# Mixer A's left and right key blocks folded by a minimum ahead of exp and transposes, and put apart again by GpSimd

## The chip, the cores and the metric

The kernel runs on one core of a Trainium2 chip. The metric is device time in microseconds (us) of one execution, the median of several runs. Engines are named as in the profile: PE (TensorE, with its weight loads as PEld), DVE (VectorE), ACT (ScalarE), POOL (GpSimd) and SP (SyncE, which issues most DMAs).

## What is computed

Two layers on 1024 tokens of 1024 channels, all in float32. Layer 0 uses mixer A, 2-D neighbourhood attention; layer 1 uses mixer B, grouped-query attention. Each is followed by a gated output projection and a gated embedding. The change concerns mixer A:

```python
rs = np.clip(r - win_r // 2, 0, rows - win_r)        # 16 rows, window of 8
cs = np.clip(c - win_c // 2, 0, GRID_W - win_c)      # 64 columns, window of 16
...
sc = jnp.einsum('bhqd,bhqnd->bhqn', qb, kg) * scale
sc = sc + bb                                         # learned bias by 2-D offset
pr = jax.nn.softmax(sc, axis=-1)
return jnp.einsum('bhqn,bhqnd->bhqd', pr, vg)
```

Each query sees 8 rows x 16 columns of keys; there are 16 heads of width 64.

## The kernel before

The host lays the tokens out in 8 tiles of 128: a tile holds all 16 rows of 8 neighbouring columns. So a query tile j sees keys of the tiles j − 1, j and j + 1 (at the two edges, j = 0 and 7, of two tiles). Of the middle tile all 8 columns lie in the window; of the left tile those with c(key) >= c(query), of the right tile those with c(key) < c(query), where c is the column within the tile. For one query and one place within a tile, thus, either the left key or the right key counts, never both.

Products of weights and activations are split into a high and a low part (three matmuls each, the helper `split3`, recorded at L315 as are all matmuls of the helper `mm`).

Mixer A walks over 16 heads x 8 query tiles, 128 steps. A step's parts, by function:

- `f_S` (scores): two matmuls into PSUM (`s`), then one DVE instruction (L674) that adds the table `tb` (bias and mask, 1e30 where a key is out) and writes `sp`, with the row's minimum `mn`. Scores are negated, so a minimum is the largest score.
- `f_E` (exp, ACT, L683): `sp` becomes exp(mn − sp) in place, with the row sums.
- `f_T` (transposes): PE transposes each 128 x 128 block of `sp` (L691) into PSUM (`t`); ACT copies it to `PTh` (L694), DVE writes the remainder to `PTl` (L695). `PTh` and `PTl` have three slots for each key tile k, for the queries of tiles k − 1, k and k + 1: slots 3k, 3k + 1, 3k + 2.
- `f_AV` (product with v, by key tile kb): two matmuls, with PTh and with PTl, over the slots of kb, into `o`. It needs the transposes of query tile kb + 1.

In step n the order is: `f_T` of n, `f_E` of n + 1, `f_S` of n + 2, and `f_AV` of n − 2. When half of a head's products are done, `head_end` brings out `Y`, and four steps later POOL multiplies it with the gate `G` (L529) and with the reciprocal row sums `rb` (L530), which come through a DMA. POOL also makes each head's table `tb` from the mask `MK` and the bias rows `u` (L649, five products). In heads 3, 7 and 11 the projection of v for the next four heads goes beside the attention (`v_items`).

All engines run their queues in order. The order is written out in the program: `mix` deals the parts of attention (`att`, with the costs CA) and of dense projections (`dense`, the next head's q and k, the gates) onto PE's queue in proportion to given costs; `pulse` after each part lets weights be staged, split into high and low (`wh` by ACT at L225, `wl` by DVE at L230) and delayed small work be issued. `QS`, `KA`, `KB` (L618 to L627) are the next head's q and k, split by ACT and DVE.

Of the kernel before, what the change touches and what calls it, by code (L numbers as in the profile page):

```python
# [21 lines left out]
NT = 8  # L22
# [3 lines left out]
NH = 16  # L26
# [4 lines left out]
CA = (1.0, 0.5, 1.25, 1.0, 0.75)  # L31
# [56 lines left out]
def lay_out(inp):  # L88
    g = {k: np.asarray(v) for k, v in inp.items()}
    W = np.empty((len(UNIT), 128, 1024), np.float32)  # L90

    def put(keys, cols, per):
        blk = cols.reshape(cols.shape[0] // 128, 128, -1).transpose(1, 0, 2)
        for u, key in enumerate(keys):
            W[UNIT[key]] = blk[:, u * per:(u + 1) * per].reshape(128, -1)

    aq, ak, av, ag = np.split(g["a_w_in"][0], 4, axis=1)
    for h in range(16):
        s = slice(h * HD, (h + 1) * HD)
        put([("aqk", h)], np.concatenate([aq[:, s], ak[:, s]], axis=1), 8)  # L100
    for q in range(4):
        put([("av", q, 0), ("av", q, 1)], av[:, q * 256:(q + 1) * 256], 4)
    bw = g["b_w_in"][0]
    bq, bk, bv, bg = bw[:, :1024], bw[:, 1024:1280], bw[:, 1280:1536], bw[:, 1536:]
    for p in range(8):
        s = slice(p * 128, (p + 1) * 128)
        put([("ag", p)], ag[:, s], 8)
        put([("bg", p)], bg[:, s], 8)
    for i in range(4):
        put([("bq", i, 0), ("bq", i, 1)], bq[:, i * 256:(i + 1) * 256], 4)  # L110
    for i in range(2):
# [24 lines left out]
    mask = np.where(ok, 0.0, BIG).astype(np.float32)  # L136

    inv = np.power(np.float32(10000.0), -np.arange(16, dtype=np.float32) * np.float32(2.0) / np.float32(32.0)).astype(np.float32)
# [12 lines left out]
    return {  # L151
        "x": tokens(g["x"][0]), "wts": W, "rpb": rpb, "gains": gains, "hgains": hg,
        "mask": mask, "rope": np.stack([cosT, sinT], axis=1),
        "gain0": gains[0].reshape(8, 128).T,
    }


@with_exitstack
def trunk(ctx, tc, x, wts, rpb, gains, hgains, mask, rope, gain0, out):
    nc = tc.nc  # L160
    sync, act, dve, pool, pe = nc.sync, nc.scalar, nc.vector, nc.gpsimd, nc.tensor

# [6 lines left out]
    ident = glob.tile([128, 128], F32, name="ident")  # L169
# [406 lines left out]
    def mixer_a():  # L576
        with ExitStack() as es:
# [4 lines left out]
            sb = es.enter_context(tc.tile_pool(name="asb", bufs=2))  # L582
            V = one.tile([128, NT, 4, 128], F32R, name="V")
            MK = one.tile([128, 5, 128], F32, name="MK")

            def dalloc():
                return pd.tile([128, 512], F32, name="d")
# [66 lines left out]
            def near(j):  # L654
                return max(j - 1, 0), min(j + 1, NT - 1)

            def f_S(h, j):
# [12 lines left out]
                else:  # L670
# [4 lines left out]
                                         in0=ps[:, :n].rearrange("p (k c) -> p k c", c=128), in1=tb,  # L675
                                         scale=1.0, scalar=1e38, op0=ALU.add, op1=ALU.min, accum_out=mn)
                SP[h, j] = (sp, mn)

            def f_E(h, j):
                k0, k1 = near(j)  # L680
                n = (k1 - k0 + 1) * 128
                sp, mn = SP[h, j]
                act.activation(sp[:, :n], sp[:, :n], AF.Exp, bias=mn, scale=-1.0, accum_out=RS[h][:, j:j + 1])  # L683

            def f_T(h, j):
                k0, k1 = near(j)
                m = k1 - k0 + 1
                sp, _ = SP.pop((h, j))
                ps = psT.tile([128, 4, 128], F32, name="t")
                for i in range(m):  # L690
                    pe.transpose(ps[:, i], sp[:, i * 128:(i + 1) * 128], ident)  # L691
                f0 = k0 * 3 + (j - k0 + 1)
                sl = slice(f0, f0 + 2 * m - 1, 2)
                act.activation(PTh[:, sl], ps[:, :m], AF.Copy)  # L694
                dve.tensor_tensor(PTl[:, sl], ps[:, :m], PTh[:, sl], ALU.subtract)  # L695

            def talloc():
                return psT.tile([128, 4, 128], F32, name="t")
# [122 lines left out]
            vs[1][1]()  # L821
            newton(4)
            sync.dma_start(MK, mask)
            for c in range(8):
                sync.dma_start(U[:, c], rpb[:, :, 7 - c:31 - c])
            for t in range(2, NT):
# [27 lines left out]
            PTh = ptp.tile([128, NT * 3, 128], F32R, name="PTh")  # L854
            PTl = ptp.tile([128, NT * 3, 128], F32R, name="PTl")
            for d in qk_items(0):
                d[0]()
                WQ.pump()
# [18 lines left out]
            for h in range(NH):  # L877
                att = []
                for j in range(NT):
# [22 lines left out]
                dense = []  # L902
                if h < NH - 1:
                    dense += qk_items(h + 1)
# [505 lines left out]
    dense_phase(1)  # L1410


NAMES = ["x", "wts", "rpb", "gains", "hgains", "mask", "rope", "gain0"]


# [13 lines left out]
```

## Time and profile before

| | |
|---|---|
| median of 3 runs | 1550.33 us (1548.04 to 1551.24) |
| profiled execution: span from first to last instruction | 1548.4 us |
| instructions in it | 24286 |
| PE busy | 1521.1 us (98%) |
| DVE busy | 1016.2 us (66%) |
| ACT busy | 874.1 us (56%) |
| POOL busy | 280.4 us (18%) |
| granted TensorE clock, mean | 0.998 |

The profile is of one execution; its own time is known by its span alone. In a row of a group of instructions stand the line, engine and operation, out<-in by the program's names, the shape and the count, then busy time and mean ns of one, then the engine's idle time just before them and what ended it. In a timeline row stand the start and the length in us, and in brackets the idle time before and its releaser; equal neighbours are merged (x3). A matmul's own length overlaps the next one's, so what PE spends is read from starts.

### The profile page before, as it was taken

The numbers are of one execution on the slowest core, as the hardware profiler recorded it, in microseconds if no ns is written. First come the engines' busy times: TensorE is split into PE (matmuls) and PEld (weight loads), VectorE is DVE, ScalarE is ACT, GpSimd is POOL, SyncE is SP. The second block draws the span as 40 slices with busy tenths as digits, with TensorE's granted clock in tenths as the row PEclk, the third lists the DMA queues.
The fourth block names the chain that finished last, engine by engine and source line by source line (L and its number), as shares of the span: only waits on it lengthen the run. The fifth ranks groups of instructions, "written<-read, shape, count | busy, mean of one in ns | idle before, by whom it ended". The sixth has DMA issues, their size and how long they took to land.

```text
span 1548.4 us, 24286 instructions
## 1 busy us (share of the span) xinstructions
PE 1521.1 (98%) x9072; PEld 1328.5 (86%) x9072; DVE 1016.2 (66%) x1990; ACT 874.1 (56%) x1757; POOL 280.4 (18%) x380
## 2 busy tenths in 40 slices
PE   8999999999999999999999999999999999999997
PEld 8888988988988888888988889989999888788886
DVE  7666576576477436557877776777777877625636
ACT  6565465465466522333567776767767767622422
POOL 1221121121121010000312122444131200000022
PEclk9999999999999999999999999999999999999999
DMA  8212122122033961232210111111101123651213
GB/s 263 97 40 72 60 80 61 52 82 79 35 99 97 355 232 55 79 139 78 75 48 22 38 48 50 41 38 56 57 27 42 62 62 116 224 197 55 74 54 131
DMA packets 90005, 138.32 MB, mean 89 GB/s; under 512 B 17056, under 2 KB 56096, under 8 KB 89888
## 3 DMA queue, kind: packets, MB, share of 16 engines
q1 hardware_dynamic: 87296, 129.17, 25.6%
q10 hardware_dynamic: 2592, 7.61, 1.4%
q8 instruction: 71, 1.16, 0.3%
q14 instruction: 46, 0.38, 0.1%
HBM read 104.13 MB, written 36.15 MB: 91 GB/s over the span
## 4 chain that ended last, share of the span: by engine, by line
PE 41%; DVE 7%; ACT 3%; issue 2%; DMA 0%; SPq 0%; ACTq 0%; DVEq 0%
PE d L315 22%; PE o L315 7%; PE t L1144 6%; PE s L315 5%; DVE PTl L1147 2%; DVE mn L1128 1%; ACT PTh L1146 1%; ACT P L1134 1%; PE t L443 1%; DVE QS L1108 1%; DVE wl L230 0%; PE t L1098 0%; DVE t L962 0%; DVE qt L963 0%; DVE Y L459 0%
## 5 line engine op out<-in xcount | busy, mean ns | idle before, releaser
L315 PE MATMUL d<-wh,HTh 128*128 128x256 f32 (+1 forms) x1096 | 369.3, 339 | 3.6 <-ACT HTh L444 1.3
L315 PE MATMUL d<-wh,HTl 128*128 128x256 f32 (+1 forms) x1096 | 363.2, 333 | 0.3 <-DVE HTl L445 0.3
L315 PE MATMUL d<-wl,HTh 128*128 128x256 f32 (+1 forms) x1096 | 362.6, 333 | 0.0
L1147 DVE TENSOR_TENSOR PTl<-t,PTh 128x512 fp32r<-128x512 f32 x256 | 164.4, 684 | 110.1 <-ACT PTh L1146 109.7
L315 PEld LDWEIGHTS d<-wh,HTh 128*128 128x128 f32 x1096 | 206.4, 189 | 26.6 <-ACT HTh L444 1.6
L315 PEld LDWEIGHTS d<-wl,HTh 128*128 128x128 f32 x1096 | 206.7, 189 | 21.7
L315 PEld LDWEIGHTS d<-wh,HTl 128*128 128x128 f32 x1096 | 206.5, 189 | 22.0 <-DVE HTl L445 0.5
L315 PE MATMUL d<-HTh,wh 128*128 128x512 f32 x504 | 205.8, 408 | 0.0
L315 PE MATMUL d<-HTh,wl 128*128 128x512 f32 x504 | 198.1, 393 | 0.0
L315 PE MATMUL d<-HTl,wh 128*128 128x512 f32 x504 | 197.5, 392 | 0.0
L1134 ACT ACTIVATE P<-s,mn 128x1024 f32<-128x1024 f32 x128 | 142.8, 1115 | 57.2 <-DVE mn L1128 56.3
L1146 ACT ACTIVATE PTh<-t 128x512 fp32r<-128x512 f32 x256 | 140.2, 594 | 45.4 <-PE t L1144 44.8
L1128 DVE TENSOR_REDUCE mn<-s 128x1 f32<-128x1024 f32 x128 | 154.8, 1209 | 11.7 <-PE s L315 11.6
L1144 PE MATMUL t<-ident,P 128*128 128x128 f32 x1024 | 137.7, 275 | 6.4 <-DVE PTl L1147 4.4
L230 DVE TENSOR_TENSOR wl<-wstage,wh 128x1024 fp32r<-128x1024 f32 x86 | 110.2, 1285 | 40.1 <-ACT wh L225 39.6
L1144 PEld LDWEIGHTS t<-ident,P 128*128 128x128 f32 x1024 | 114.6, 140 | 22.5 <-DVE PTl L1147 16.6
L315 PE MATMUL s<-KA,QS 128*128 128x512 f32 (+2 forms) x384 | 133.5, 402 | 0.0
L315 PE MATMUL s<-KB,QS 128*128 128x512 f32 (+2 forms) x384 | 121.7, 371 | 0.0
L315 PE MATMUL o<-PTh,V 128*128 128x256 f32 (+2 forms) x672 | 118.8, 288 | 1.2 <-DVE Y L459 0.9
L315 PE MATMUL o<-PTl,V 128*128 128x256 f32 (+2 forms) x672 | 119.0, 288 | 0.1
L695 DVE TENSOR_TENSOR PTl<-t,PTh 128x384 fp32r<-128x384 f32 (+1 forms) x128 | 66.6, 520 | 74.7 <-ACT PTh L694 73.4
L315 PEld LDWEIGHTS d<-HTh,wl 128*128 128x128 f32 x504 | 94.6, 188 | 21.7
(201 smaller groups left out, 2486.0 us busy)
## 6 DMA issues: line engine op xcount, KB each, us to landing
wstage<-in_wts SPq DMA_DIRECT2D x92, 512.0 KB
pp<-ppD SPq DMA_DIRECT2D x32, 256.0 KB
X<-in_x SPq DMA_DIRECT2D x15, 512.0 KB
rb<-rD SPq DMA_DIRECT2D x56, 128.0 KB
ppD<-th SPq DMA_DIRECT2D x20, 256.0 KB
xD<-X SPq DMA_DIRECT2D x8, 512.0 KB
X<-xD SPq DMA_DIRECT2D x8, 512.0 KB
yD0h<-rb SPq DMA_DIRECT2D x14, 256.0 KB
```

The lines of the kernel that those rows point to most:

```text
L230: eng.tensor_tensor(lo[:, c:c + n], s[:, c:c + n], hi[:, c:c + n], ALU.subtract)
L315: pe.matmul(ps, a, b, start=first, stop=last, skip_group_check=True)
L443: pe.transpose(ps[:, k], xn[:, (4 * c + k) * 128:(4 * c + k + 1) * 128], ident)
L695: dve.tensor_tensor(PTl[:, sl], ps[:, :m], PTh[:, sl], ALU.subtract)
L1108: post.add(DQ, lambda: dve.tensor_tensor(qs[oth], raw[own], qs[own], ALU.subtract))
L1128: dve.tensor_reduce(mn, ps, axis=AX.X, op=ALU.min)
L1134: act.activation(p, ps, AF.Exp, bias=mn, scale=-1.0, accum_out=RS[h, hf][:, t:t + 1])
L1144: pe.transpose(ps[:, i], p[:, k * 128:(k + 1) * 128], ident)
L1146: act.activation(PTh[:, ks, c], ps, AF.Copy)
L1147: dve.tensor_tensor(PTl[:, ks, c], ps, PTh[:, ks, c], ALU.subtract)
```

## The change

For the inner tiles (j = 1 to 6), `f_S` ends with one more DVE instruction that overwrites the left block of `sp` by the minimum of left and right block. Where a key is out, its entry is 1e30, so the minimum is that of the one that counts. `f_E` then takes 256 columns (folded block and middle block) in place of 384, and `f_T` two transposes in place of three: the middle block goes to its slot 3j + 1, the folded block to one of two new slots behind the others (24 + j % 2). Then POOL multiplies the folded block by two 0/1 blocks (`SIDE`, a new input loaded once behind `MK`) and writes the products to slot 3j − 1 (left key tile) and 3j + 3 (right key tile), one instruction for PTh and one for PTl. `f_AV` is issued a step later, for n − 3 in place of n − 2; the last three products follow step 127. The row sums are the same: exp of an entry of 1e30 is zero.

```diff
@@ f_S
                 SP[h, j] = (sp, mn)
+                if 0 < j < NT - 1:
+                    dve.tensor_tensor(sp[:, 0:128], sp[:, 0:128], sp[:, 256:384], ALU.min)
@@ f_E
-                k0, k1 = near(j)
-                n = (k1 - k0 + 1) * 128
+                n = 256
@@ f_T
-                k0, k1 = near(j)
-                m = k1 - k0 + 1
                 sp, _ = SP.pop((h, j))
                 ps = psT.tile([128, 4, 128], F32, name="t")
-                for i in range(m):
-                    pe.transpose(ps[:, i], sp[:, i * 128:(i + 1) * 128], ident)
-                f0 = k0 * 3 + (j - k0 + 1)
-                sl = slice(f0, f0 + 2 * m - 1, 2)
-                act.activation(PTh[:, sl], ps[:, :m], AF.Copy)
-                dve.tensor_tensor(PTl[:, sl], ps[:, :m], PTh[:, sl], ALU.subtract)
+                inner = 0 < j < NT - 1
+                for i in range(2):
+                    c = 1 - i if inner else i
+                    pe.transpose(ps[:, i], sp[:, c * 128:(c + 1) * 128], ident)
+                k0 = near(j)[0]
+                f0 = 3 * j + 1 if inner else k0 * 3 + (j - k0 + 1)
+                f1 = 3 * NT + j % 2 if inner else f0 + 2
+                sl = slice(f0, f1 + 1, f1 - f0)
+                act.activation(PTh[:, sl], ps[:, :2], AF.Copy)
+                dve.tensor_tensor(PTl[:, sl], ps[:, :2], PTh[:, sl], ALU.subtract)
+                if inner:
+                    def apart():
+                        for pt in (PTh, PTl):
+                            pool.tensor_tensor(pt[:, 3 * j - 1:3 * j + 4:4],
+                                               pt[:, f1:f1 + 1].to_broadcast([128, 2, 128]), SIDE, ALU.mult)
+                    apart()
@@ the steps
-                    if n >= 2:
-                        att += av_and_v(*steps[n - 2])
+                    if n >= 3:
+                        att += av_and_v(*steps[n - 3])
@@ the end
-                    att += [(lambda: f_AV(NH - 1, NT - 2), CA[4]), (lambda: f_AV(NH - 1, NT - 1), CA[4])]
+                    att += [(lambda k=k: f_AV(NH - 1, k), CA[4]) for k in range(NT - 3, NT)]
```

More of the change, by code (lines that the diff above doesn't have):

```diff
@@ L136, in lay_out @@
     mask = np.where(ok, 0.0, BIG).astype(np.float32)
+    sides = np.stack([c[:, None] >= c[None, :], c[:, None] < c[None, :]], axis=1).astype(np.float32)
     inv = np.power(np.float32(10000.0), -np.arange(16, dtype=np.float32) * np.float32(2.0) / np.float32(32.0)).astype(np.float32)
@@ L152, in lay_out @@
         "x": tokens(g["x"][0]), "wts": W, "rpb": rpb, "gains": gains, "hgains": hg,
-        "mask": mask, "rope": np.stack([cosT, sinT], axis=1),
+        "mask": mask, "sides": sides, "rope": np.stack([cosT, sinT], axis=1),
         "gain0": gains[0].reshape(8, 128).T,
@@ L158, in trunk @@
 @with_exitstack
-def trunk(ctx, tc, x, wts, rpb, gains, hgains, mask, rope, gain0, out):
+def trunk(ctx, tc, x, wts, rpb, gains, hgains, mask, sides, rope, gain0, out):
     nc = tc.nc
@@ L584, in mixer_a @@
             MK = one.tile([128, 5, 128], F32, name="MK")
+            SIDE = one.tile([128, 2, 128], F32, name="SIDE")
             def dalloc():
@@ L685, in f_T @@
             def f_T(h, j):
-                k0, k1 = near(j)
-                m = k1 - k0 + 1
                 sp, _ = SP.pop((h, j))
                 ps = psT.tile([128, 4, 128], F32, name="t")
-                for i in range(m):
-                    pe.transpose(ps[:, i], sp[:, i * 128:(i + 1) * 128], ident)
-                f0 = k0 * 3 + (j - k0 + 1)
-                sl = slice(f0, f0 + 2 * m - 1, 2)
-                act.activation(PTh[:, sl], ps[:, :m], AF.Copy)
-                dve.tensor_tensor(PTl[:, sl], ps[:, :m], PTh[:, sl], ALU.subtract)
+                inner = 0 < j < NT - 1
[11 more added lines that the diff above has]
+                        for pt in (PTh, PTl):
+                            pool.tensor_tensor(pt[:, 3 * j - 1:3 * j + 4:4], pt[:, f1:f1 + 1].to_broadcast([128, 2, 128]), SIDE,
+                                               ALU.mult)
+                    apart()
             def talloc():
@@ L823, in mixer_a @@
             sync.dma_start(MK, mask)
+            sync.dma_start(SIDE, sides)
             for c in range(8):
@@ L853, in mixer_a @@
             ptp = es.enter_context(tc.tile_pool(name="ptp", bufs=1))
-            PTh = ptp.tile([128, NT * 3, 128], F32R, name="PTh")
-            PTl = ptp.tile([128, NT * 3, 128], F32R, name="PTl")
+            PTh = ptp.tile([128, NT * 3 + 2, 128], F32R, name="PTh")
+            PTl = ptp.tile([128, NT * 3 + 2, 128], F32R, name="PTl")
             for d in qk_items(0):
@@ L1410, in trunk @@
     dense_phase(1)
-NAMES = ["x", "wts", "rpb", "gains", "hgains", "mask", "rope", "gain0"]
+NAMES = ["x", "wts", "rpb", "gains", "hgains", "mask", "sides", "rope", "gain0"]
 def kernel(**inputs):
```

## The prediction, made before the changed kernel ran

> **What bounds the kernel now.** I read the page first, then the busy time of the engines by stage, then the groups of instructions and the waits of mixer A, and last the timelines of single steps.
>
> ```profile
> PE 1521.1 (98%) x9072; PEld 1328.5 (86%) x9072; DVE 1016.2 (66%) x1990; ACT 874.1 (56%) x1757; POOL 280.4 (18%) x380
> PEclk9999999999999999999999999999999999999999
> ```
>
> TensorE is busy for 98% of the span, and its clock is granted in full in all 40 slices. DVE is at 66%, ACT at 56%, POOL at 18%. The change touches mixer A alone; its 128 attention steps run from 59.8 to 523 us:
>
> ```profile
> 59.80:523.00 463.20, 461.64 (x2652) 403.46 (x2651) 293.86 (x661) 274.94 (x615) 82.09 (x98) 1.00 0.26 82
> 207.70:256.50 48.80, 48.80 (x261) 41.78 (x259) 35.88 (x81) 32.46 (x73) 12.15 (x14) 1.00 0.25 74
> 256.50:304.00 47.50, 47.50 (x324) 44.08 (x323) 20.88 (x49) 19.82 (x46) 4.98 (x7) 1.00 0.09 29
> ```
>
> The columns are the stretch and its length, then the busy time (and count) of PE, PEld, DVE, ACT and POOL. PE is busy for 461.6 of 463.2 us, so PE's stream of instructions sets the length of the stage. The second row holds two normal heads (24.4 us each, some 3 us a step): DVE is at 35.9 of 48.8 us, ACT at 32.5, POOL at 12.2. The third row lies around one of the three heads in which v of the next four heads is projected as well; there DVE is at 20.9 of 47.5 us and has room. So 13 of the 16 heads are normal, and in them DVE is the engine next to PE.
>
> ```profile
> PEld t L691 <- ACT sp L683: 7.0, 20, 1.1
> ```
>
> This is PE's only wait of weight in the stage: the weight load of a transpose waits for an exponential, 20 times and 7.0 us in all, much of it under the matmul that still runs. The transposes themselves sat idle for another 1.4 us (their row is below).
>
> **The change part by part.** In each of the 96 inner steps (16 heads, query tiles 1 to 6) three key blocks become two.
>
> *PE: one transpose less in each inner step.* The group's mean of 275 ns is not its price, since a matmul starts before the one ahead has ended:
>
> ```profile
> L691 PE MATMUL t<-ident,sp 128*128 128x128 f32 x352 | 60.2, 275 | 1.4 <-ACT sp L683 1.0
> 207.54 0.49 PE L691 MATMUL t<-ident,sp 128*128 128x128 f32 x3
> 207.78 0.42 PE L315 MATMUL s<-KA,QS 128*128 128x384 f32 x1
> 208.04 0.34 PE L315 MATMUL s<-KB,QS 128*128 128x384 f32 x1
> ...
> 250.55 0.38 PE L691 MATMUL t<-ident,sp 128*128 128x128 f32 x2
> 250.69 0.42 PE L315 MATMUL s<-KA,QS 128*128 128x384 f32 x1
> 250.95 0.34 PE L315 MATMUL s<-KB,QS 128*128 128x384 f32 x1
> ```
>
> Both cases are followed by the same two score matmuls of 384 columns. From the first transpose to the second score matmul it takes 208.04 − 207.54 = 0.50 us with three transposes and 250.95 − 250.55 = 0.40 us with two; the merged durations differ by 0.49 − 0.38 = 0.11. I take 0.105 us: 96 × 0.105 = **10.1 us less**, on the path. By the mean of 275 ns it would be 26 us, which the starts rule out. No other PE instruction goes or comes: the products with v are the same ones, a step later.
>
> *ACT: exp and the copy of the transposes lose 128 columns each.*
>
> ```profile
> L683 ACT ACTIVATE sp<-sp,mn 128x384 f32<-128x384 f32 x96 | 58.9, 613 | 8.2 <-DVE mn L674 7.5
> L694 ACT ACTIVATE PTh<-t 128x384 fp32r<-128x384 f32 x96 | 47.1, 491 | 56.2 <-PE t L691 55.4 <-PE s L315 0.3
> ...
> L683 ACT ACTIVATE sp<-sp,mn 128x256 f32<-128x256 f32 x31 | 15.7, 505 | 4.7 <-DVE mn L674 4.7
> L694 ACT ACTIVATE PTh<-t 128x256 fp32r<-128x256 f32 x31 | 11.9, 383 | 10.9 <-PE t L691 10.6
> ```
>
> That is 613 − 505 + 491 − 383 = 216 ns a step, 20.7 us of ACT in all. ACT is beside the path; the saving counts only where PE waits for an exponential, so between 0 and 7.0 + 1.4 us. The 1.4 us in the row of the transposes is certainly on the path. I take **1 us less**.
>
> *DVE: a minimum more, a shorter residual.* The minimum is a tensor_tensor of 128 columns from SBUF; the nearest row of that form is one of mixer B, on DVE, below, median 285 ns. The residual goes from 556 to 412 ns.
>
> ```profile
> L695 DVE TENSOR_TENSOR PTl<-t,PTh 128x384 fp32r<-128x384 f32 x96 | 53.4, 556 | 64.9 <-ACT PTh L694 64.0
> L695 DVE TENSOR_TENSOR PTl<-t,PTh 128x256 fp32r<-128x256 f32 x31 | 12.8, 412 | 9.7 <-ACT PTh L694 9.5
> ...
> L963 POOL TENSOR_TENSOR qt<-qt,tab x24: 726/740/1220, 791.5 to 1209.7; 128x256 f32<-128x256 f32 x24
> L963 DVE TENSOR_TENSOR qt<-th,tab x8: 281/285/498, 727.8 to 748.5; 128x128 f32<-128x128 f32 x8
> ```
>
> Net 285 − (556 − 412) = +141 ns a step, 12 × 0.141 = 1.7 us in two normal heads: DVE goes from 35.9 to 37.6 us while PE shrinks from 48.8 to 48.8 − 12 × 0.105 = 47.5. By itself that is covered by DVE's idle time. The minimum also stands between scores and exp, but exp becomes 108 ns shorter, so exp ends only about 0.18 us later where DVE was the last to come.
>
> *POOL: two products of 256 columns in each inner step.* The same size, also with a broadcast operand, is the POOL row just above: median 740 ns, at best 726, at worst 1220. So 1.48 us a step, 24 × 0.74 = 17.8 us in two normal heads. With the tables and the gate products that POOL does already (12.2 us) it is 29.9 of 47.5 us busy: loaded, not full. All of it would lie beside PE, if nobody waits for it. Three do:
>
> 1. The product with v of tile j − 1 now needs POOL's blocks of step j. The change issues it a step later, about where tile j's product stood before. The tightest place that I find is the head after a v head:
>
> ```profile
> 186.42 0.54 DVE L695 TENSOR_TENSOR PTl<-t,PTh 128x384 fp32r<-128x384 f32 x1
> 189.45 0.56 DVE L695 TENSOR_TENSOR PTl<-t,PTh 128x384 fp32r<-128x384 f32 x1
> ...
> 193.48 0.28 PE L315 MATMUL o<-PTh,V 128*128 128x256 f32 x1
> ```
>
> The residual of step (4,2) ends at 186.96, that of (4,3) at 190.01, and the product that stood a step later began at 193.48: 3.5 us of room. POOL has there: the products of (4,2) until 187.7; the two gate products that a head's end puts in front of step (4,3), 2 × 1.30, until 190.3; the two of (4,3), until 191.8. That leaves 1.7 us. If each POOL product took 0.9 instead of 0.74 us and the gate products met DVE as below (1 us more), nothing would be left. I take 0 to 1 us at each of the three such heads.
>
> 2. The gate products wait for a DMA (rb), and POOL's queue would stand still behind it:
>
> ```profile
> 224.93 1.30 POOL L529 TENSOR_TENSOR Y<-Y,G 128x512 f32<-128x512 f32 x1 [1.34 <-DVE Y L459]
> 231.98 1.29 POOL L530 TENSOR_TENSOR Y<-Y,rb 128x512 f32<-128x512 f32 x1 [5.74 <-DMA rb<-rD]
> ```
>
> Now POOL runs ahead: it starts the first product as soon as Y is there and waits 5.74 us for rb, which it has 7.05 us after that start. In the new order the pair stands behind the side products of the step that is four steps (12 us) after the half head's last product with v, so the 7 us have mostly passed when it comes to the front. I bound the wait by 0 and 2 us, inside the room of point 1 in all but the tight places, and take nothing.
>
> 3. ACT's copy and DVE's residual of step n + 2 overwrite the folded slot that POOL reads in step n. That is two steps (about 6 us) for 1.48 us of work, or 4.1 us with gate products ahead: covered, and if it is not, ACT's queue stops and with it the exponentials.
>
> *DVE and POOL hold each other up.* The trace shows this wherever both read two SBUF operands:
>
> ```profile
> 184.18 2.31 DVE L230 TENSOR_TENSOR wl<-wstage,wh 128x1024 fp32r<-128x1024 f32 x1
> 188.27 0.69 DVE L623 TENSOR_TENSOR KB<-th,KA 64x512 fp32r<-64x512 f32 x1
> 226.71 1.21 DVE L230 TENSOR_TENSOR wl<-wstage,wh 128x1024 fp32r<-128x1024 f32 x1
> 245.28 0.86 DVE L623 TENSOR_TENSOR KB<-th,KA 64x512 fp32r<-64x512 f32 x1
> ...
> 183.09 2.33 POOL L529 TENSOR_TENSOR Y<-Y,G 128x512 f32<-128x512 f32 x1 [9.10 <-DVE Y L459]
> 244.63 3.49 POOL L649 TENSOR_TENSOR tb<-MK,u 128x128 f32<-128x128 f32 x5 [1.97 <-DVE mn L674]
> 277.72 2.38 POOL L649 TENSOR_TENSOR tb<-MK,u 128x128 f32<-128x128 f32 x5 [29.61 <-DVE mn L674]
> ```
>
> At 183.09 a gate product takes 2.33 us instead of 1.30 (224.93), and the weight residual beside it 2.31 instead of 1.21 (226.71): 1.10 us lost on DVE to a 512-column product. At 244.63 five table products of 128 columns take 3.49 us instead of 2.38 (277.72), and DVE's KB beside them 0.86 instead of 0.69 (188.27): 0.17 us lost. Between the two sizes, a 256-column product costs DVE 0.17 + (1.10 − 0.17) × 128/384 = 0.48 us when it is met. With 24 of them in two normal heads the bounds are 0 and 11.5 us; DVE is idle or at PSUM operands for much of the time, so I take half of them met, at three quarters of the full wait: 24 × 0.5 × 0.36 = 4.3 us. DVE is then at 37.6 + 4.3 = 41.9 of 47.5 us: still below PE, but its queue runs late by some tenths of a us in bursts, and the steps in which an exponential was just in time make PE wait. I charge 0.25 us for each of the 13 normal heads (bounds 0 and 0.8): **3.3 us more**, and 0.8 us for point 1.
>
> *The rest.* One more DMA (128 KB, the side factors) stands on SP's queue in the start stage, ahead of the bias rows. What it delays is bounded by an issue on that queue:
>
> ```profile
> 240.34 0.54 SPq L643 DMA_DIRECT2D u<-U  x1
> ```
>
> 0 to 0.5 us, once; head 0's own projection lies between the table and the first step, so I take nothing. Both tails end with one more product with v before the last two dense items; same work, same order of releases: nothing.
>
> **Sum.** −10.1 − 1 + 3.3 + 0.8 = −7.0 us on the profiled span of 1548.4: 1541.4. The median of the runs shown, 1550.33, is 1.9 us above that span, so **1543.3 us**.
>
> **The rivals.**
>
> *A, the pure gain.* POOL and DVE stay inside their room everywhere: −10.1 − 1 to −2.5, so 1537.7 to 1539.2. For it: DVE's 26% of idle time. Against it: DVE's queue already runs late in places.
>
> *B, the gain is eaten by late exponentials.* The charge per normal head is 0.6 to 0.8 us; the sum is −10.1 − 1 + 13 × 0.6 to 0.8 + 0.8 to 1.5, −2.5 to +0.8: 1547.8 to 1551.1 us. For it: the 20 waits of PE for an exponential above. Against it: ACT gets 216 ns a step back, just there.
>
> *C, DVE becomes the bound in the normal heads: slower.* Its place is DVE's queue in the 13 normal heads, its price the wait that each POOL product puts on DVE. Two normal heads then take 37.6 + 24w us. At w = (48.8 − 37.6)/24 = 0.47 us this is the length of before; above it the kernel is slower. At w = 0.6 it is 52.0, or 3.2 us × 6.5 pairs = 21 us more: 1571. At w = 0.74, when every product blocks DVE for its whole length, 55.4, 43 us more: 1593. For it: the 1.10 us of a 1.30 us product. Against it: the 0.17 us of a 0.48 us product, and the half of DVE's instructions that read PSUM and don't meet POOL (the residuals at 0.41 and 0.56 us keep their length everywhere in the group above). The Trainium skill, SBUF — State Buffer, section "Who interferes with whom", speaks against the change here: it has a DVE instruction with two SBUF inputs and a GpSimd instruction that reads SBUF exclude each other for the whole instruction, the second one fully blocked. By that rule w goes up to the 0.74 us. The trace agrees for the large product and shows less for the small ones, so I give it less than one chance in five.
>
> *D, the change does not do what it says:* the transpose is hidden behind something else. Then nothing changes, 1550. The two timelines of PE speak against it.
>
> **How the numbers follow.** A measurement of this kernel can tell about 0.2% (3.1 us) from no change. Forecast, 1540 to 1547: 0.50. A: 0.14. B: 0.15. C: 0.17. D: 0.04. Faster by over 0.2%: forecast and A, 0.64. Within: B and D, 0.19. Slower: C, 0.17. The range runs from A's lower end to the first part of C, 1537 to 1555, leaving out most of C and little below A.
>
> **What would show it.** Right: transposes x256, the stage some 7 us shorter, POOL's new products at 0.74 to 0.95 us, DVE at 40 to 43 us in two normal heads, PE's idle time before o and t in the stage below 6 us. Wrong: PE waiting for PTh or PTl from POOL (point 1), ACT's copy waiting for POOL (point 3), or exponentials that wait for a mn that comes over 1 us later than now (B, C). If the new products take over 1.1 us, the room at the tight places is gone.

## The result, and the profile after

The changed kernel takes 1568.11 us (median of 4 runs, 1565.85 to 1569.89), the kernel before on the same chip 1549.55: ratio 1.012, 95% interval 1.0108 to 1.0132. It is slower by 18.6 us; 1543.3 had been forecast, and the range ended at 1555.

First the engines' busy time on the page of the changed kernel, to be held against the same line of before:

```profile
PE 1515.5 (97%) x8976; PEld 1317.9 (84%) x8976; DVE 1075.7 (69%) x2086; ACT 853.7 (55%) x1757; POOL 433.2 (28%) x572
```

The 96 transposes are gone (9072 matmuls have become 8976), yet the profiled span is 1564.1 us. Then the busy time by stage, the whole of mixer A and two normal heads (5 and 6), in the columns of before:

```profile
59.60:538.68 479.08, 455.59 (x2545) 391.12 (x2544) 353.04 (x754) 254.24 (x613) 234.38 (x290) 1.00 0.24 79
207.14:258.80 51.66, 48.69 (x249) 40.25 (x249) 44.27 (x94) 30.20 (x74) 30.22 (x39) 1.00 0.23 70
```

Before, PE was busy for 461.6 of 463.2 us of the stage; now for 455.6 of 479.1. So PE's own work shrank by 6 us, and its idle time grew from 1.6 to 23.5 us. Heads 5 and 6 take 51.7 us where they took 49.1 (201.5 to 250.6 us of the trace before), and DVE is busy for 44.3 of them. (The other two such pairs up to head 10 take 49.8 and 50.7 us.) What PE waits for stands in the waits of the stage (total us, times, longest):

```profile
PEld t L694 <- ACT sp L686: 34.7, 35, 3.4
ACT sp L686 <- DVE sp L681: 32.9, 25, 3.1
ACT sp L686 <- DVE mn L676: 23.2, 11, 2.8
PE t L694 <- ACT sp L686: 22.2, 26, 3.1
...
POOL Y L531 <- DMA rb<-rD: 3.2, 4, 1.3
...
ACT PTh L699 <- POOL PTl L704: 0.6, 1, 0.6
```

The transposes' own wait for exponentials grew from 1.0 to 22.2 us, and the exponentials wait for DVE: for the minimum (`sp`) or the scores' instruction (`mn`). No product with v waits for POOL. (The gate products come in every second head, 28 in the stage.) The groups of the changed kernel show who keeps DVE:

```profile
L704 POOL TENSOR_TENSOR PTh<-PTh,SIDE 128x256 fp32r<-128x256 f32 x96 | 80.1, 834 | 211.0 <-ACT PTh L699 211.0
L704 POOL TENSOR_TENSOR PTl<-PTl,SIDE 128x256 fp32r<-128x256 f32 x96 | 78.7, 819 | 33.6 <-DVE PTl L700 33.6
...
L694 PE MATMUL t<-ident,sp 128*128 128x128 f32 x256 | 51.2, 282 | 22.5 <-ACT sp L686 22.2
...
L681 DVE TENSOR_TENSOR sp<-sp 128x128 f32<-128x128 f32 x96 | 42.2, 440 | 3.3
L625 DVE TENSOR_TENSOR KB<-th,KA 64x512 fp32r<-64x512 f32 x32 | 37.1, 1159 | 0.5
L624 DVE SCALAR_TENSOR_TENSOR QS<-th,QS 64x512 fp32r<-64x512 f32 x32 | 33.2, 1038 | 4.5 <-ACT QS L620 3.5
```

and the same two splits in the kernel before:

```profile
L623 DVE TENSOR_TENSOR KB<-th,KA 64x512 fp32r<-64x512 f32 x32 | 24.4, 763 | 0.7
L622 DVE SCALAR_TENSOR_TENSOR QS<-th,QS 64x512 fp32r<-64x512 f32 x32 | 23.5, 735 | 4.9 <-ACT QS L618 3.9
```

DVE's splits of the next head's q and k (four instructions of 512 columns, twice a head: QS, KB, KA and the copy of KB) became longer by half. A timeline of one such place, head 6 of the changed kernel, in the order DVE, POOL, ACT, PE:

```profile
252.42 1.15 DVE L624 SCALAR_TENSOR_TENSOR QS<-th,QS 64x512 fp32r<-64x512 f32 x1
253.58 1.69 DVE L625 TENSOR_TENSOR KB<-th,KA 64x512 fp32r<-64x512 f32 x1
255.30 1.41 DVE L626 CAST KA<-KA 64x512 fp32r<-64x512 f32 x1
...
252.29 0.74 POOL L704 TENSOR_TENSOR PTl<-PTl,SIDE 128x256 fp32r<-128x256 f32 x1
252.98 1.74 POOL L530 TENSOR_TENSOR Y<-Y,G 128x512 f32<-128x512 f32 x1
254.80 1.63 POOL L531 TENSOR_TENSOR Y<-Y,rb 128x512 f32<-128x512 f32 x1
...
258.12 0.51 ACT L686 ACTIVATE sp<-sp,mn 128x256 f32<-128x256 f32 x1 [2.77 <-DVE mn L676]
...
258.77 0.44 PE L694 MATMUL t<-ident,sp 128*128 128x128 f32 x2 [0.28 <-ACT sp L686]
```

QS, KB and KA last 4.25 us here. Where they met nothing in the kernel before it was 0.69 + 0.69 + 0.42 = 1.80:

```profile
259.43 0.69 DVE L622 SCALAR_TENSOR_TENSOR QS<-th,QS 64x512 fp32r<-64x512 f32 x1
260.14 0.69 DVE L623 TENSOR_TENSOR KB<-th,KA 64x512 fp32r<-64x512 f32 x1
260.87 0.42 DVE L624 CAST KA<-KA 64x512 fp32r<-64x512 f32 x1
```

In the rows of head 6 POOL does the product on PTl and both gate products beside them. The exponential then waits 2.77 us, and PE for it. In the kernel before most of the gate products lay apart from the splits: POOL was idle and took the first one as soon as Y was there (224.93, 1.1 us ahead of head 6 and seven us ahead of the second product, in the prediction's rows). In the changed kernel that one starts 8.8 us into head 6 (2.8 us with the step later alone, an experiment below), and the one of the second half, in the rows above, 21.1 us into it, where it was 8.6.

Where the 15.7 us between the two spans lie, from the starts of the transposes in the traces (a head goes from its first transpose to the next head's):

| us | before | after |
|---|---|---|
| up to the first transpose of the attention | 60.0 | 59.6 |
| head 0 | 20.1 | 22.8 |
| heads 1 to 14 | 418.5 | 430.7 |
| head 15, up to its last transposes | 23.4 | 25.6 |
| behind them | 1026.4 | 1025.4 |

The start differs by up to 2.5 us between profiled executions of all kernels (59.6 to 62.1), so the experiments are compared by their medians and by heads 1 to 14, called H below (418.5 before, 430.7 after). Beside H stands the sum S of the lengths of DVE's 120 splits of q and k between 60 and 540 us of the trace (72.3 us before, 107.5 after), and how many of them overlap a gate product (9 and 34). (In the kernel with the copies on ACT only 60 of the 120 are left on DVE; its S is left out.)

### The profile page after: what moved, and what is told of

It is laid out like the page before. It is cut to its first block, busy times and chain, and to the rows that moved or that the text cites. A ratio compares the mean times of both kernels' runs of the same rounds, so it can differ in the third digit from the quotient of the medians.

```text
span 1564.1 us, 24489 instructions
## 1 busy us (share of the span) xinstructions
PE 1515.5 (97%) x8976; PEld 1317.9 (84%) x8976; DVE 1075.7 (69%) x2086; ACT 853.7 (55%) x1757; POOL 433.2 (28%) x572
## 3 DMA queue, kind: packets, MB, share of 16 engines
q8 instruction: 71, 1.16, 0.3%
## 4 chain that ended last, share of the span: by engine, by line
PE 43%; DVE 6%; ACT 2%; issue 2%; DVEq 0%; ACTq 0%
PE d L316 23%; PE o L316 7%; PE t L1156 6%; PE s L316 6%; DVE PTl L1159 1%; DVE mn L1140 1%; ACT PTh L1158 1%; PE t L444 1%; ACT P L1146 0%; PE t L1110 0%; DVE wl L231 0%; DVE QS L1120 0%; DVE t L974 0%; DVE qt L975 0%; DVE KB L1051 0%
## 5 line engine op out<-in xcount | busy, mean ns | idle before, releaser
L1140 DVE TENSOR_REDUCE mn<-s 128x1 f32<-128x1024 f32 x128 | 154.7, 1209 | 11.8 <-PE s L316 11.7
L704 POOL TENSOR_TENSOR PTh<-PTh,SIDE 128x256 fp32r<-128x256 f32 x96 | 80.1, 834 | 211.0 <-ACT PTh L699 211.0
L1156 PEld LDWEIGHTS t<-ident,P 128*128 128x128 f32 x1024 | 114.8, 140 | 21.1 <-DVE PTl L1159 15.4
```

Of the source, the lines that this page charges most:

```text
L704: pool.tensor_tensor(pt[:, 3 * j - 1:3 * j + 4:4], pt[:, f1:f1 + 1].to_broadcast([128, 2, 128]), SIDE, ALU.mult)
L1140: dve.tensor_reduce(mn, ps, axis=AX.X, op=ALU.min)
L1156: pe.transpose(ps[:, i], p[:, k * 128:(k + 1) * 128], ident)
```

## Experiments

| kernel | us | ratio to before, 95% interval | H | S (beside a gate product) |
|---|---|---|---|---|
| fold alone | 1544.79 | 0.9961 (0.9946 to 0.9976) | 410.7 | 74.5 (9) |
| changed, no products | 1553.89 | 1.0023 (1.0012 to 1.0033) | 416.1 | 75.4 (13) |
| before, step later only | 1562.73 | 1.0081 (1.0066 to 1.0096) | 425.9 | 78.1 (23) |
| before, products beside | 1551.94 | 1.0009 (1.0000 to 1.0019) | 418.8 | 92.7 (11) |
| changed, on time | 1567.85 | 1.0101 (1.0081 to 1.0121) | 430.4 | 90.8 (9) |
| step later, split of Y earlier | 1554.71 | 1.0028 (1.0018 to 1.0037) | 421.4 | 77.7 (19) |
| changed, split of Y earlier | 1565.01 | 1.0091 (1.0076 to 1.0106) | 425.9 | 108.1 (34) |
| changed, copies by ACT | 1575.46 | 1.0165 (1.0148 to 1.0182) | 440.4 | |
| changed, POOL only fills | 1552.46 | 1.0015 (1.0006 to 1.0025) | 416.5 | 77.8 (14) |
| changed, POOL copies | 1558.86 | 1.0056 (1.0041 to 1.0071) | 424.6 | 88.6 (28) |
| changed, half the products | 1563.22 | 1.0084 (1.0067 to 1.0101) | 426.8 | 94.3 (27) |
| changed, minimum from PSUM | 1567.22 | 1.0109 (1.0094 to 1.0124) | 429.2 | 108.2 (39) |
| changed, no minimum | 1562.84 | 1.0080 (1.0065 to 1.0095) | 427.1 | 112.4 (39) |
| changed, gate products a step earlier | 1558.31 | 1.0050 (1.0034 to 1.0066) | 421.4 | 89.1 (18) |
| changed, gate products a step later | 1561.18 | 1.0064 (1.0048 to 1.0081) | 424.8 | 92.0 (7) |
| changed, gate products apart | 1558.80 | 1.0052 (1.0037 to 1.0067) | 421.9 | 89.8 (5) |
| fills only, split of Y earlier | 1547.78 | 0.9984 (0.9975 to 0.9994) | 413.4 | 76.8 (13) |
| fold in heads 3, 7, 11 | 1549.00 | 0.9992 (0.9983 to 1.0002) | 416.5 | 74.8 (9) |

**The change in its parts.** *No products:* from head 1 on nothing is put apart.

```diff
-                    apart()
+                    if h == 0:
+                        apart()
```

> The changed kernel with POOL's side products issued for head 0 alone; later heads read the blocks of head 0 (the side blocks are left out of the computation). Fold, minimum, two transposes and the later product with v stay. Theory T1 (POOL's products and DVE's instructions with two SBUF operands or of the copy kind hold each other up, DVE's queue runs late, and exp and the transposes with it): the loss is gone and the transposes' saving is there, 1539 to 1543 us, DVE's KB at 0.69 and the minimum at 0.29 us. Theory T2 (the minimum on the chain from the scores to exp is what makes PE wait): still above 1558 us. Theory T3 (products with v and the v projection a step later cost it): still above 1558 us.

1553.89: the products carry 14.2 us of the loss. They are not the whole of it: little of the transposes' saving is there, and none of the three theories gives this time. Part of what is left lies in head 0, which keeps its products (24.4 us, 20.1 before); H is 2.4 us below before.

*Step later only,* the kernel before with this edit (and, as in the change, the last three products behind step 127):

```diff
-                    if n >= 2:
-                        att += av_and_v(*steps[n - 2])
+                    if n >= 3:
+                        att += av_and_v(*steps[n - 3])
```

> The kernel before with the products with v a step later (n - 3 for n - 2) and nothing else of the change. T1 and T2: 1549 to 1551 us, no change. T3: above 1558 us.

1562.73: the edit that I had costed at nothing takes 12.7 us by itself. H grows by 7.4; a further 5.9 lie in head 15, where PE stood still once for 2.6 us in the profiled execution, behind ACT and a DMA, and went on at a lower clock (0.66 granted from 520 to 530 us); that execution is the slowest of the four (1565.73). ACT's queue in head 6 shows a cause, first with the step later, then before:

```profile
246.58 1.05 ACT L225 ACTIVATE wh<-wstage 128x1024 fp32r<-128x1024 f32 x1
247.53 0.62 ACT L526 ACTIVATE rb<-Y 128x512 fp32r<-128x512 f32 x1
248.05 0.62 ACT L618 ACTIVATE QS<-th 64x512 fp32r<-64x512 f32 x1
248.68 0.63 ACT L619 ACTIVATE KA<-th 64x512 fp32r<-64x512 f32 x1
249.33 0.49 ACT L694 ACTIVATE PTh<-t 128x384 fp32r<-128x384 f32 x1
```

```profile
240.89 1.05 ACT L225 ACTIVATE wh<-wstage 128x1024 fp32r<-128x1024 f32 x1
241.84 0.62 ACT L618 ACTIVATE QS<-th 64x512 fp32r<-64x512 f32 x1
242.47 0.63 ACT L619 ACTIVATE KA<-th 64x512 fp32r<-64x512 f32 x1
243.12 0.49 ACT L694 ACTIVATE PTh<-t 128x384 fp32r<-128x384 f32 x1
```

Everything that is counted from a half head's last product with v moves too. The split of Y (L526, 0.62 us of ACT) lands ahead of the splits of q and k and of the next exponential.

*Products beside,* the kernel before with `SIDE` loaded and POOL's products into a spare tile that nobody reads:

```diff
+                    for pt, o in ((PTh, 0), (PTl, 1)):
+                        pool.tensor_tensor(SPARE[:, 2 * o:2 * o + 2],
+                                           pt[:, 3 * j + 1:3 * j + 2].to_broadcast([128, 2, 128]), SIDE, ALU.mult)
```

> The kernel before with POOL's two 256-column products in each inner step added, read from PTh and PTl and written to a spare tile that nobody reads: three blocks, three transposes and no minimum, as before, and the order of the products with v as before. Only POOL's load is added. T1: slower by 8 to 25 us (1558 to 1575), with DVE's QS, KB and KA stretched as in the changed kernel (1.06, 1.19, 0.77 us). T2 and T3: within 2 us of before.

1551.94, 1.9 us above before, where the theory of the hold-up alone had 8 to 25. The hold-up on DVE is there and costs next to nothing, as the group of KB and PE's wait show:

```profile
L626 DVE TENSOR_TENSOR KB<-th,KA 64x512 fp32r<-64x512 f32 x32 | 33.5, 1046 | 0.7
...
PEld t L694 <- ACT sp L686: 7.6, 23, 1.1
```

KB takes 1046 instead of 763 ns and S grows by 20 us, but PE's wait stays at 7.6 us (7.0 before). So the order of the kernel before has room for this, and the changed one has not.

*Fold alone:* the kernel without products, its products with v back at n − 2.

> Minimum and two transposes as in the changed kernel, but the products with v at n - 2 as before and POOL's side products for head 0 alone (left out for heads 1 to 15, which read the blocks of head 0). Theory A (the shift of the products with v, and of all that hangs on them, by a step makes exponentials late; POOL's products add to it through DVE's queue; the transposes' saving itself is real): 1538 to 1542 us, PE's stalls at the transposes within 3 us of before. Theory B (the minimum by itself makes exponentials late): 1548 us or more.

1544.79. A normal head takes 23.8 us instead of 24.5, one with v 41.0 instead of 41.7. The time is 2.8 us above theory A's range and below theory B's. Each part set on top of the one ahead of it, H goes from 418.5 to 410.7 by the fold (−7.8), to 416.1 by the step later (+5.4) and to 430.7 by the products (+14.6). By the medians it is −5.9, +9.1 and +14.2; the medians take in the start and the heads 0 and 15.

**The order.** *On time:* the whole change, its products with v at n − 2.

> The whole change but the shift: fold, POOL's side products, and the products with v at n - 2 as before. Theory A: most of the loss goes; what remains is PE waiting for POOL's products ahead of o, 0 to 12 us by the room of 1.5 to 4 us that the products with v had: 1541 to 1555 us. Theory B: within 4 us of the changed kernel (1564 to 1572).

1567.85, a miss: without the step's shift the loss only changes its place. The waits of PE name POOL now:

```profile
PEld o L316 <- POOL PTl L704: 9.5, 13, 1.7
PEld o L316 <- POOL PTh L704: 7.3, 6, 2.5
```

So the shift is needed for the products, and costs something of its own. H also holds more than the waits here: the granted clock is 0.83 in four windows of 10 us (from 130, 205, 370 and 455 us), which by 10 × 0.17 each comes to an estimate of 6.8 us; in the changed kernel's H it is granted in full.

*Split of Y earlier,* in the kernel with only the step later, and in the changed one:

```diff
-YS = (11, 11)
+YS = (6, 11)
```

> The kernel before with the products with v a step later (this alone took 1562.7 us) and the split of Y into high and low (L526 on ACT, L527 on DVE) five parts, about a step, earlier after the gate products (YS 6 in place of 11), so that it falls where it fell before. Theory A1 (it is this split that now falls on the step in which ACT has a weight split and the next head's q and k ahead of the exponential): 1551 to 1557 us. Theory A2 (it is the outcome of Y itself, L495 and L459, or the order of the v projection): still 1560 or more.

> The changed kernel with the split of Y five parts earlier (YS 6). A1: 4 to 10 us faster than the changed kernel (1558 to 1564). A2: within 3 us of it.

1554.71 and 1565.01. In the first, 8.0 of the 12.7 us go; of the two spans' difference (1563.9 to 1552.8) 4.5 us lie within H, 6.2 in head 15 and 1.3 in the start. In the changed kernel it is 3.1 us, between the two theories' ranges. So the split's place carries much of the shift's loss in the kernel before, and little in the changed one.

**What about the products costs.** *Minimum from PSUM,* a DVE instruction of as many columns with one operand from PSUM:

```diff
-                    dve.tensor_tensor(sp[:, 0:128], sp[:, 0:128], sp[:, 256:384], ALU.min)
+                    dve.scalar_tensor_tensor(sp[:, 0:128], ps[:, 256:384], 0.0, sp[:, 0:128], op0=ALU.mult, op1=ALU.add)
```

> The changed kernel with the minimum replaced by a DVE instruction on as many columns that reads one operand from PSUM (the scores' right block times zero, plus the left block of sp), so that DVE's queue stays as long and only its pair of SBUF operands goes. It leaves out the right-hand keys. Open is why GpSimd's products cost some 14 us here (1553.9 us without them, 1568.1 with them) and 1.9 us beside the kernel before. P, the minimum and the products hold each other up in SBUF, and the exponential behind the minimum comes late: 1554 to 1561 us. Q, the minimum's place in DVE's queue matters, not its operands: the copies and splits of DVE are what the products lengthen, 1564 to 1570 us. R, the products delay their own readers (products with v): 1565 to 1570 us.

*No minimum:* the two lines of the minimum are gone. (In both kernels the mask leaves the right block out.)

> The changed kernel without the minimum; the left and middle block alone are used, so it leaves out the right-hand keys. P (minimum against products, on the way to the exponential): 1552 to 1558 us, at or below the changed kernel without products. Q (the products lengthen DVE's copies and splits, whatever stands in the chain): only DVE's 0.29 us a step are gained, 1560 to 1566 us.

1567.22 and 1562.84. The instruction from PSUM takes 291 ns where the minimum took 440, and nothing is gained; without any, 5.3 us. Both times are in the ranges of the theory that the products lengthen DVE's copies and splits. So the minimum's meeting with the products is not what costs.

*Only fills* and *copies* in place of the products:

```diff
-                            pool.tensor_tensor(pt[:, 3 * j - 1:3 * j + 4:4], pt[:, f1:f1 + 1].to_broadcast([128, 2, 128]), SIDE, ALU.mult)
+                            pool.memset(pt[:, 3 * j - 1:3 * j + 4:4].bitcast(F32), 0.125)
```

> The changed kernel with each of GpSimd's products replaced by a fill of the same 256 columns with a constant: the order, the waits for the folded slot's neighbours and the readers stay, GpSimd's two SBUF operands go. It leaves out the putting apart. P (two SBUF readers at once hold each other up): DVE's instructions return to the lengths they have without products, 1553 to 1558 us. R (the products delay their readers, whatever they read): 1563 to 1570 us.

```diff
+                            pool.tensor_copy(pt[:, 3 * j - 1:3 * j + 4:4], pt[:, f1:f1 + 1].to_broadcast([128, 2, 128]))
```

> The changed kernel with each of GpSimd's products replaced by a copy of the folded block into both slots: one SBUF operand read in place of two, order and readers as before. It leaves out the multiplication by SIDE. If any reading by GpSimd holds DVE's copies of q and k up, in proportion to its length: 1556 to 1566 us, with KB's remainder well above its 0.71 us of the write-only form. If it takes two operands on each side: 1551 to 1555 us, as write-only (1552.5), and KB's remainder near 0.71 us.

1552.46 and 1558.86, beside 1568.11 with products. The groups of the filling kernel:

```profile
L681 DVE TENSOR_TENSOR sp<-sp 128x128 f32<-128x128 f32 x96 | 33.7, 351 | 3.3
L704 POOL MEMSET PTh<- 128x256 f32 x96 | 30.8, 321 | 63.4 <-PE o L316 63.4
...
L625 DVE TENSOR_TENSOR KB<-th,KA 64x512 fp32r<-64x512 f32 x32 | 22.9, 715 | 0.5
```

KB is back at 715 ns, 1159 with products. The fills are also shorter (0.32 us) and read nothing that they would wait for, so order and length change with the reading. The copies, 0.50 us and one operand, lie between: KB at 942.

*Half the products:* from head 1 on that on PTh alone.

```diff
-                        for pt in (PTh, PTl):
+                        for pt in (PTh, PTl) if h == 0 else (PTh,):
```

> The changed kernel with the product on PTh alone from head 1 on; it leaves out the putting apart of PTl. If the loss grows with the number of products (1553.9 us without, 1568.1 with all): 1559 to 1563 us. If the queue before the exponential has room for one product a step and not for two: 1553 to 1557 us. If one is as bad as two: 1565 to 1569 us.

1563.22, just above the range of the proportional case: half of the products cost two thirds of the loss.

*Copies by ACT:* the KA and KB copies (`dve.tensor_copy`) become `act.activation(..., AF.Copy)`.

> The changed kernel with the two copies of KA and KB (60 of 0.42 us alone, 0.77 and 0.57 us in the changed kernel) done by ACT in place of DVE. T1: DVE gets some 40 us back in the stage and meets POOL less; ACT takes 37 us more; 1553 to 1564 us, faster than the changed kernel by 4 to 15. T2: within 4 us of the changed kernel, since the minimum stays; T3 likewise.

1575.46, a miss. Each copy that leaves DVE puts some 0.63 us into ACT's queue, and the transposes wait for exponentials for 28.9 us, 22.2 in the changed kernel.

**Where the gate products lie.** That POOL's work costs 2 us in one order and 14 in the other left its place open. In the traces, 34 of the 120 splits meet a gate product in the changed kernel and last 1.39 us each, the others 0.70; before, 9 do. Three kernels move the gate products and leave the rest of POOL's work as it is:

```diff
-FIN = (4, 4)
+FIN = (3, 4)
```

> The changed kernel with the two gate products (and the split of Y that is counted from them) a step earlier in GpSimd's queue, 3 us or so ahead of the splits of q and k. If the meeting of gate products and splits carries most of the 14 us: 1553 to 1561 us, with fewer than 15 splits beside a gate product. If GpSimd's work costs the same wherever it lies: 1564 to 1569 us. If the reciprocal row sums come too late for it, GpSimd stands still with the products of PTh and PTl behind it, PE waits for them, and it is 1565 us or slower.

```diff
-FIN = (4, 4)
-YS = (11, 11)
+FIN = (5, 4)
+YS = (6, 11)
```

> The changed kernel with the two gate products a step later; the split of Y stays where it is (6 parts behind them in place of 11). They begin some 3 us behind where they are, at the end of the splits of q and k. If the meeting carries the loss: 1555 to 1563 us. If GpSimd's work costs the same wherever it lies: 1564 to 1569 us.

```diff
-YS = (11, 11)
+YS = (6, 11)
...
-                            later.add(FIN[0], fin)
...
+                                later.add(FIN[0] - 1, fin.gate)
+                                later.add(FIN[0] + 1, lambda fin=fin: fin(False))
```

> The changed kernel with the gate product (which needs no row sums) a step earlier and the product with rb a step later, the split of Y where it is: neither then lies on the splits of q and k, and GpSimd is held up at most 1.7 us at once. If the meeting carries the loss: 1552 to 1560 us, the lowest of the three. If GpSimd's work costs the same wherever it lies: 1564 to 1569 us.

1558.31, 1561.18 and 1558.80: 7 to 10 us of the 14 go, though POOL does the same work as in the changed kernel; S falls from 107.5 to about 90. All three times are in the range of the meeting, though not each sign of it: the first has 18 splits beside a gate product where fewer than 15 were expected, and the last is no faster than the first. (The first moves the split of Y a step ahead as well, which by itself was worth 3.1 us; the other two leave it about where it was.) The step earlier pays in another place; its waits in the stage have

```profile
POOL Y L531 <- DMA rb<-rD: 32.8, 12, 4.7
...
PEld o L316 <- POOL PTl L704: 5.4, 7, 0.9
```

POOL stands still for 32.8 us behind the row sums (3.2 in the changed kernel), with the products behind it, and PE waits for one now and then. Over the kernels with fold and shift H rises with S in the main: 413.4 to 416.5 where S is 75 to 78, 421.4 to 424.8 where it is 89 to 92, 426.8 to 430.7 where it is 94 to 108. Two do not follow: 425.9 at 108.1 with the split of Y earlier, and 427.1 at 112.4 without the minimum. So S is a part of what sets H, and not all of it. From the kernel without products to the changed one it is 14.6 us of H for 32.1 us of S, 0.45 for each. In the order of before it was 0.3 us of H for 20.4.

**Together.** *Fills only, split of Y earlier:* both edits at once.

> Both causes taken away together: GpSimd only fills (it leaves out the putting apart), and the split of Y is issued about a step earlier. If the place of the split (8 us of the shift's 12.7 in the kernel before) and the reading of the products are the whole loss, this comes near the fold alone (1544.8 us): 1544 to 1549 us. If the place of the split matters only beside long exponentials of three blocks: 1551 to 1554 us, as the write-only form is.

1547.78, inside what the two causes would leave, 3.0 above the fold alone.

*Fold in heads 3, 7 and 11,* at n − 2:

```diff
+            FOLDED = (3, 7, 11)
...
+            def folded(h, j):
+                return h in FOLDED and 0 < j < NT - 1
```

> The kernel before with the fold, the two transposes and GpSimd's products in heads 3, 7 and 11 only (18 steps of 128), where the projection of v makes a step 5.2 us long in place of 3.1 us; the products with v stay at n - 2. If a long step covers the products and DVE's queue has room there: 18 transposes of 0.105 us are gained, 1.9 us, so 1547.5 to 1550 us by a kernel before of 1550.5. If the order of ACT's and DVE's queue in those heads is as delicate as elsewhere: 1551 to 1555 us.

1549.00: the three pairs of a head with v and the one behind it take 214.9 instead of 216.8 us, the 1.9 us expected, but the median is not told apart from before. It is the only folded version with the whole computation that is not slower.

## Why the prediction was wrong, by its own steps

*One transpose less, −10.1 us: right.* The fold alone shows 0.7 us less in most heads, by 6 × 0.105 = 0.63, and 7.8 over the 14 heads of H, by 8.8.

*ACT's relief, −1 us: wrong in sign.* PE's waits for exponentials grew from 1.0 to 2.7 us with the fold alone, to 11.8 with the step later and to 22.2 with the products.

*DVE's minimum: mis-sized.* 285 ns were assumed, and it took 351 to 363 without products and 440 with them. DVE's two normal heads come to 38.3 us without products (207.6 to 255.9 us of that trace), by 37.6 worked out.

*POOL's products: right in length, wrong in what they push.* 0.82 to 0.83 us by 0.74; two normal heads 30.2 us by 29.9. No product with v waits for them, so the 0.8 us of point 1 did not come, and point 3, the slot, cost 0.6 us. Point 2 looked only at POOL's wait for rb (0 to 2 us, taken at nothing; the rows show 3.2 in all). It overlooked that the pair, no longer ahead in an idle POOL, would come down on the splits of q and k. This is one of the two steps that failed at a large price (the other is the shift, below): the three moved kernels give 7 to 10 us for it, the first of them 3.1 less if the split of Y is worth there what it was by itself.

*DVE and POOL hold each other up: the hold-up nearly right, its price not.* 4.3 us were taken for two normal heads; it is 44.3 − 38.3 = 6.0. But the charge for it, 0.25 us a normal head with 0.8 as the bound, was guessed: 3.3 us in all. It is 14.6 / 14 = 1.04 us a head, 14.2 us by the medians. By the rows of DVE alone it was still covered: 44.3 of 51.7 us are busy. A share of busy time did not tell that the exponential of each step waits for the one instruction at the end of a burst.

*"The same ones, a step later", nothing: wrong.* In H it is 5.4 us with the fold and 7.4 in the kernel before; by the medians 9.1 and 12.7. The step counted PE's instructions, which are the same, and not what is timed from them on ACT, DVE and POOL.

*The rivals.* B named the mechanism, late exponentials, and bounded it by 0.8 us a head. C was on the right side by another mechanism: DVE was to be full from w = 0.47 us a product; measured is (44.3 − 37.6) / 24 = 0.28, by which C would have given a faster kernel. Its rule from the Trainium skill, SBUF — State Buffer, section "Who interferes with whom", says also that a DVE instruction with two SBUF inputs is disturbed by a GpSimd instruction that reads SBUF and not by one that only writes it. The fills agree (KB 715 ns, 0.69 us where it meets nothing). That the two shut each other out for the whole instruction, as the prediction has it from there, the rows of head 6 above bear out: KB, 0.69 us alone, ends 0.55 us behind the end of the first gate product (255.27 and 254.72); the second gate product, 1.30 us alone, ends 1.16 us behind KB; KA, 0.42 us alone, 0.28 us behind that. Each does all but 0.14 us of its work after the other has ended. In all 43 cases of this trace in which QS or KB outlasts an instruction of POOL beside it, it ends 0.54 us or more behind it. The KB of 0.86 us that the prediction read as less than the rule is no exception: it ends 0.55 us behind the first of the table products beside it (246.14 and 245.59). What failed in C is its step from the rule to w: a product blocks DVE only for what is left of it when DVE's instruction comes, and not at all where it is itself the second, so w stayed at 0.28.

What stays open: why the changed order has so little room that 0.45 us of each us of S is lost, in which part the split of Y and in which the fold's minimum takes it; and whether the stand in head 15 belongs to the step's shift or to that execution; and what makes up the 4 to 7 us of the products' loss that are left when the gate products are moved.

## What to carry to other kernels

When a step is moved, follow everything that is counted from it on every engine: here the split of Y on ACT and the gate products on GpSimd moved with products on PE that were "the same". An engine that is idle takes its next instruction as soon as that is ready; give it work, and what stood early in time falls to its written place, so ask what it meets there. On an engine that is busy for 86% of the time (44.3 of 51.7 us) what counts is the last instruction of a burst that another engine waits for, not the sum.

## What the runs showed of the hardware

A long wait of PE can cost more than its length. In head 0 of the changed kernel the transposes waited 3.08 us for an exponential; PE's timeline there, and the windows of 10 us (the third number from the end is the granted clock):

```profile
67.35 0.44 PE L694 MATMUL t<-ident,sp 128*128 128x128 f32 x2 [3.08 <-ACT sp L686]
...
71.55 0.63 PE L316 MATMUL d<-HTl,wh 128*128 128x512 f32 x1
71.98 0.47 PE L316 MATMUL d<-HTh,wl 128*128 128x512 f32 x1
```

```profile
60.00:70.00 10.00, 6.92 (x33) 5.62 (x33) 7.30 (x17) 4.08 (x13) 4.67 (x6) 0.94 0.14 52
70.00:80.00 10.00, 9.65 (x47) 7.79 (x46) 7.68 (x18) 5.52 (x15) 4.67 (x6) 0.89 0.20 72
```

From one start to the next a 512-column matmul takes 71.98 − 71.55 = 0.43 us here, where 0.23 is usual, and the clock is granted at 0.94 and 0.89 in two windows: 10 × (0.06 + 0.11) = 1.7 us, on top of the wait. Before, both windows stand at 1.00. It does not always come: in the kernel with the gate products apart PE waited 3.08 us at the same place (66.0 to 69.1), and both windows stand at 1.00; nor did it come behind the changed kernel's next waits of 2.2 us. And shorter ones can do: in the on-time kernel two waits of 0.87 and 0.75 us within 3 us (131 and 132 us) stand ahead of the window at 0.83. Such stretches also lie in H of the changed kernel with the split of Y earlier, with half the products and with the minimum from PSUM (one each) and with the copies by ACT (two), by the same working 1.7 us each. The Trainium skill, TensorE: Matmul & The Clock Gate, section "Part 1: The HAM clock gate", has the clock halved after about 3.4 us without work and given back after about as long of sustained work; the trace agrees in kind (half the clock from 68.7 to 72.1 us), but with waits shorter than that.

The copies KA and KB, which read one SBUF operand, are held up by POOL's products as well: KA takes 1.41 us at 255.30 where 0.42 is usual.

Of two instructions of DVE and POOL that meet in this way, the second does all but 0.14 us of its work after the first has ended: the rows of head 6, worked out above under the rivals.
